# When the weight sums of the Mixer's last product are made, and which engine splits the next weights

## The chip, the cores and the metric

The kernel runs on one core of a Trainium2 chip. The metric is the device time of one execution in microseconds (us), as the median of several runs. Five engines work side by side and meet only at semaphores: TensorE (PE, with its weight loads as PEld), VectorE (DVE), ScalarE (ACT), GpSimd (POOL) and SyncE (SP). Each takes its instructions strictly in the order of its own queue. SP and POOL issue the DMAs here, each on a queue of its own.

## The reference

Two layers, 512 tokens, 1024 features. Each layer is three steps, each with a layer norm (LN) behind it:

```
x = LN(alpha*x + 0.5*swiglu_1(x))
x = LN(alpha*x + Mixer(x))
x = LN(alpha*x + 0.5*swiglu_2(x))

Mixer: zq, zf, zi, zg, zu, zv, za, zb = split(x @ w_in)
  o = hgrn2(q, k, i, log f)               # chunked gated recurrence, 4 heads
  o = o * rsqrt(mean(o^2) + eps) * g * silu(zg);   y_a = o @ w_branch_a
  v = LN(gelu(zv));  mixed = causal 128x128 mixing of v
  y_b = (gelu(zu) * mixed) @ w_branch_b
  y = sigmoid(za)*y_a + sigmoid(zb)*y_b
  return y @ w_out                        # the Mixer's last product
```

All of it is float32. `swiglu` has a hidden width of 2816.

## The kernel before, in words

**Three products for one.** A float32 operand is cut in two by `split` (L125 to L127): ACT copies it, rounded, into `hi`, and DVE subtracts to get `lo`. A product is then three matmuls: hi by hi, hi by lo, lo by hi. `weights` (L129) does this for a weight block of 128x1024: SP loads it into a `raw` tile (four of them), then comes the split, into two of ten `w` tiles or, with `early`, into two of the 34 big tiles of the tag `h`.

**Seven products for eight.** Large products use a scheme of 2x2 blocks with seven products and with sums of blocks on both sides. For the class `Seven` (L295) the sums of weights are made in DRAM, ahead of use: `sums_in_dram` (L308) yields six steps, a copy from DRAM to DRAM and an adding DMA for each of the three kinds of sums (`t13`, `t2`, `t4`). They are issued by POOL, and an add waits on POOL until its copy has landed, the next copy until the add has:

```
for of, kw in ((copy, {}), (add, {"accum_op": ALU.add})):
    for k in ks:
        tc.keep_in_program_order(nc.gpsimd.dma_start(*of(k), **kw))
    yield 0.0, next(gap)
```

Between two steps lies a gap in nanoseconds from a list. For the Mixer's last product that is `OUT_SUMS` (L141), and `w_out` is the source.

**Who sets the order.** `Flow` (L50) keeps a planned clock. Every matmul loop ticks it, and side tasks, written as generators, run one step when they are due: `flow.add(gen, delay)` starts one, `flow.finish` runs one to its end. So the program order, and with it each engine's queue, is woven from a main line and side tasks. Within it a list scheduler may move an instruction ahead on its engine; what `keep_in_program_order` names stays in place.

**The Mixer** (L864 on), main line:
1. queries and gates; `x_sums` forms sums of x; `all_sums` queues the DRAM sums for `two_tokens` and then, as `column_sums` (L932), those for the columns (`zt`, 1 MB each);
2. `columns(4)`: u. A call of `columns` (L941) is seven products with weights loaded by SP;
3. `two_tokens` (L882): i and v by the seven-product scheme. Its order on PE: X and C with b and t1 (`iX`, `iC`), then the copies of X and C out of PSUM by ACT (L905), then `iX` with t2 on the same bank, then c, t3 and t4;
4. v's moments (L1262 to L1272), with four roots `vr` on POOL (`rstd_of`, L185), one for each 128 tokens;
5. `columns(0)` to `columns(3)`: the two gates. Side tasks here: `all_out` with `head_out` (L1161) for pairs of heads (transposes `kt`, states `st`, outputs `o`, roots `rs` on POOL, scaling by DVE, transposes `ot`), and `spatial`, the mixing of v;
6. the loop over k that multiplies both branches, L1313: the products `y`, DVE's gating and sums, and the sums of y for the last product (`activation_sums`, `later`);
7. `so.run` (L424), the last product: b and t2 by P1, P6, P5 (`pA`, `pB`, `pC`), c by P2 and P3, d by P7 and P4 (`pB`, `pF`). DVE adds each bank into x (`add_to`, L200), and `norm` makes LN: mean and square sum, a root on POOL, two passes by DVE (L230, L231). Then PE transposes the new x (`tr`, L177) for the next FFN.

The next FFN begins with four weight blocks, a and b for the blocks 10 and 21, loaded and split by `next_weights` within the Mixer. Before the change, the first two come in the loop over k (at k = 2), the other two in `run`, behind three splits of d.

`first_weights` in `run` is called behind the loads of d for the first two ks (`two_d`, L412, with `early`) and a third:

```
for k in ks[0:early_d]:
    self.two_d(k, True)
if few:
    self.two_d(ks[early_d])
    first = first_weights()
```

`few` is true for the Mixer's last product alone. The sums of `w_out` are started ahead of `two_tokens`, with a delay of 1000 ns.

Of the kernel before, what the change touches and what calls it, by code (L numbers as in the profile page):

```python
# [40 lines left out]
NF = DFF // P  # L41
# [42 lines left out]
def trunk(ctx: ExitStack, tc, x_in, xt_in, w13, w2, w_in, w_iv, w_z, w_br, w_out, ln_g, ln_b, lb_in, hgn, sgg, sgb, sgws,  # L84
# [35 lines left out]
    def pin(ins):  # L120

        if pinned[0]:
            tc.keep_in_program_order(ins)

    def split(hi, lo, src):  # L125
        pin(S.activation(hi, src, AF.Copy))  # L126
        pin(V.tensor_tensor(lo, src, hi.bitcast(F32), op=ALU.subtract))  # L127

    def weights(src, name, early=False):  # L129

        raw = wk.tile([P, D], F32, tag="raw", name=f"r_{name}", bufs=NRAW)
        pin(nc.sync.dma_start(raw, src))
        if early:
            hi, lo = (slot(f"{c}_{name}", F32R).rearrange("p a t -> p (a t)") for c in "hl")
        else:
            hi, lo = (wk.tile([P, D], F32R, tag="w", name=f"{c}_{name}", bufs=NW) for c in "hl")
        split(hi, lo, raw)
        return hi, lo

    SUM_GAP = 7000.0  # L140
    OUT_SUMS = [10000.0, 28000.0, 10000.0, 16000.0, 10000.0, 0.0]  # L141
    X_GAP = 2500.0
# [152 lines left out]
    class Seven:  # L295
# [88 lines left out]

        def two(self, name, loads, keys, early=False):

            m = len(keys)
            raw = wk.tile([P, 2, 512], F32, tag="raw", name=f"r_{name}", bufs=NRAW)
            if len(loads) == 1:
                nc.sync.dma_start(raw[:, 0:m], loads[0])  # L390
            else:
                for z, d in enumerate(loads):
                    nc.sync.dma_start(raw[:, z], d)
            if early:
                hi, lo = (slot(f"{v}_{name}", F32R) for v in "hl")
            else:
                hi, lo = (wk.tile([P, 2, 512], F32R, tag="w", name=f"{v}_{name}", bufs=NW) for v in "hl")
            split(hi[:, 0:m], lo[:, 0:m], raw[:, 0:m])
            for z, key in enumerate(keys):
                self.ops[key] = hi[:, z], lo[:, z]  # L400
# [10 lines left out]

        def two_d(self, k, early=False):  # L412
            self.two(f"d{k}", [self.t13[k][:, 1], self.t4[k]], [("t3", k), ("t4", k)], early)

# [9 lines left out]
        def run(self, c, ln, last, due, first_weights):  # L424
# [64 lines left out]
            for k in ks[0:early_d]:  # L489
                self.two_d(k, True)  # L490
            if few:
# [231 lines left out]

    def ffn_weights(l, i, which=(0, 1)):

        return [[weights(w13[l, i, c + j], f"{n}{j}", True) for n, c in (("a", 0), ("b", NF))]
                for k in FRONT for j in (k + z * NH2 for z in which)]
# [136 lines left out]
    def mixer(l, lb, om, first, next_weights):  # L864
# [372 lines left out]
        def all_out():  # L1237
            for h in range(0, NH, 2):
# [17 lines left out]
                        tril.unsqueeze(1).broadcast_to([P, NH, P]), op=ALU.mult)  # L1256
        flow.finish(in_dram)
        so = Seven(lambda k: w_out[l, k], list(range(KT // 2)), [], "o")
        out_sums = flow.add(so.sums_in_dram(so.order, 4, OUT_SUMS), 1000.0)
        two_tokens()  # L1260
        late.append(flow.add(all_out(), 4000.0))
# [48 lines left out]
        for t in late:  # L1310
            flow.finish(t)
        wbr = [None, None]
        for k in range(4):  # L1313
            for a in range(2):
# [12 lines left out]
            if k < 2:  # L1327
                so.later(k, 0)
                so.later(k, 2)
            if k == 2:  # L1330
                first = next_weights(0)
        flow.finish(out_sums)
        return so.run(1.0 / ALPHA, (l, 1), False, [], lambda: first + next_weights(1))

# [51 lines left out]
    for l in range(DEPTH):  # L1386
        first = ffn(l, 0, first, lambda: mixer_weights(l))
        if l == 0:
            flow.finish(prep)
        first = mixer(l, lb, om, first, lambda z: ffn_weights(l, 1, (z,)))  # L1390
        first = ffn(l, 1, first, (lambda: ffn_weights(l + 1, 0)) if l < DEPTH - 1 else None)
# [98 lines left out]
```

## Time and profile before

| | us |
|---|---|
| median of 3 runs | 2027.38 |
| lowest and highest | 2026.88, 2029.39 |
| the profiled execution | 2028.06 |
| its span, first to last instruction | 2026.3 |
| PE busy | 2002.0 |
| DVE busy | 1699.7 |
| ACT busy | 1072.8 |
| POOL busy | 398.6 |

The span is the time between the first and the last instruction; 1.8 us of the execution lie around it. Mean granted clock of PE is 0.994 of full speed. Views of the profile used here: busy time by engine, by group of instructions and by stretch of time; who waited for whom (the engine that waited, its line, the releaser, total, times, longest); and the timeline (start, duration, engine, line, operation, output from inputs; in brackets the idle time before it and what ended it). Names are those of the program's tiles: `h_` and `l_` are the high and low part, `r_` the raw load; digits at their ends are left out. A busy PE need not be at its peak: its ends are modelled. The Mixer of layer 0 runs from about 352 to 675 us, that of layer 1 from about 1359 to 1683.

### The profile page before, as it was taken

The numbers are of one execution on the slowest core, as the hardware profiler recorded it, in microseconds if no ns is written. First come the engines' busy times: TensorE is split into PE (matmuls) and PEld (weight loads), VectorE is DVE, ScalarE is ACT, GpSimd is POOL, SyncE is SP. The second block draws the span as 40 slices with busy tenths as digits, with TensorE's granted clock in tenths as the row PEclk, the third lists the DMA queues.
The fourth block names the chain that finished last, engine by engine and source line by source line (L and its number), as shares of the span: only waits on it lengthen the run. The fifth ranks groups of instructions, "written<-read, shape, count | busy, mean of one in ns | idle before, by whom it ended". The sixth has DMA issues, their size and how long they took to land. (4 is left out here: it accounts for less than half of the span.)

```text
span 2026.3 us, 34947 instructions
## 1 busy us (share of the span) xinstructions
PE 2002.0 (99%) x13552; PEld 1861.0 (92%) x13552; DVE 1699.7 (84%) x2519; ACT 1072.8 (53%) x1577; POOL 398.6 (20%) x541
## 2 busy tenths in 40 slices
PE   9999999999999999999999999999999999999998
PEld 8999888897998899998899999888889989999986
DVE  8888888976769798888789889889677698988886
ACT  5545665336544464556555456652465454554563
POOL 0322003212200133210123320022222001322101
PEclk9999999999999999999999999999999999999999
DMA  6999786887636389987649997778876363899774
GB/s 237 273 263 241 242 268 228 199 230 237 174 125 214 130 217 255 269 232 259 207 147 283 269 243 260 254 229 206 236 226 166 116 228 113 240 248 265 239 253 135
DMA packets 184006, 448.75 MB, mean 221 GB/s; under 512 B 20480, under 2 KB 20608, under 8 KB 183840
## 3 DMA queue, kind: packets, MB, share of 16 engines
q1 hardware_dynamic: 118656, 271.70, 39.0%
q0 software_dynamic: 65184, 174.82, 35.8%
q8 instruction: 106, 1.74, 0.3%
q14 instruction: 60, 0.49, 0.1%
HBM read 424.42 MB, written 164.63 MB: 291 GB/s over the span
## 5 line engine op out<-in xcount | busy, mean ns | idle before, releaser
L126 ACT ACTIVATE h_pa<-ra 128x1024 fp32r<-128x1024 f32 x80 | 84.5, 1057 | 191.9 <-DVE ra L624 185.9
L322 POOL DMA_DIRECT2D t<-in_w_dram x176 | 145.6, 898 | 202.7 <-DMA t<-in_w_dram 113.4
L127 DVE TENSOR_TENSOR l_pc<-rc,h_pc 128x1024 fp32r<-128x1024 f32 x80 | 97.7, 1222 | 47.7 <-ACT h_pc L126 47.7
L322 POOL DMA_DIRECT2D t<-t x104 | 56.4, 543 | 288.2 <-DMA t<-in_w_dram 260.3
L126 ACT ACTIVATE h_b<-r_b 128x1024 fp32r<-128x1024 f32 (+1 forms) x69 | 71.7, 1042 | 63.5 <-DMA r_b<-t 35.6
L127 DVE TENSOR_TENSOR l_c<-r_c,h_c 128x1024 fp32r<-128x1024 f32 x60 | 72.4, 1222 | 38.9 <-ACT h_c L126 38.1
L127 DVE TENSOR_TENSOR l_b<-r_b,h_b 128x1024 fp32r<-128x1024 f32 (+1 forms) x69 | 83.1, 1205 | 25.2 <-ACT h_b L126 24.9
L127 DVE TENSOR_TENSOR l_pa<-ra,h_pa 128x1024 fp32r<-128x1024 f32 x80 | 97.7, 1221 | 2.6 <-ACT h_pa L126 2.6
L126 ACT ACTIVATE h_c<-r_c 128x1024 fp32r<-128x1024 f32 x60 | 62.6, 1056 | 58.5 <-PE pC L381 33.4
L644 PE MATMUL fC<-xs4h,l_pd 128*128 128x256 f32 x320 | 90.6, 283 | 0.0
L644 PE MATMUL fA<-xh,h_pc 128*128 128x256 f32 x320 | 90.6, 283 | 0.0
L644 PE MATMUL fC<-xs1h,h_pt 128*128 128x256 f32 x320 | 90.6, 283 | 0.0
L644 PE MATMUL fX<-xs2h,l_pa 128*128 128x256 f32 x320 | 90.6, 283 | 0.0
L644 PE MATMUL fX<-xh,h_pa 128*128 128x256 f32 x320 | 90.6, 283 | 0.0
L644 PE MATMUL fC<-xs1h,l_pt 128*128 128x256 f32 x320 | 90.6, 283 | 0.0
L644 PE MATMUL fX<-xl,h_pa 128*128 128x256 f32 x320 | 90.6, 283 | 0.0
L644 PE MATMUL fX<-xs2h,h_pa 128*128 128x256 f32 x320 | 90.6, 283 | 0.0
L644 PE MATMUL fX<-xh,l_pa 128*128 128x256 f32 x320 | 90.6, 283 | 0.0
L644 PE MATMUL fC<-xs1l,h_pt 128*128 128x256 f32 x320 | 90.6, 283 | 0.0
L644 PE MATMUL fX<-xs3h,l_pb 128*128 128x256 f32 x320 | 90.6, 283 | 0.0
L644 PE MATMUL fX<-xs3h,h_pb 128*128 128x256 f32 x320 | 90.6, 283 | 0.0
L644 PE MATMUL fA<-xl,h_pc 128*128 128x256 f32 x320 | 90.6, 283 | 0.0
(480 smaller groups left out, 8018.4 us busy)
## 6 DMA issues: line engine op xcount, KB each, us to landing
t<-in_w_dram POOLq DMA_DIRECT2D x88, 512.0 KB, 9.6
t<-t POOLq DMA_DIRECT2D x104, 256.0 KB, 5.0
t<-in_w_dram POOLq DMA_DIRECT2D x88, 256.0 KB, 7.0
r_c<-in_w_dram SPq DMA_DIRECT2D x44, 512.0 KB, 4.9
r_d<-t SPq DMA_DIRECT2D x88, 256.0 KB, 3.9
ra<-in_w_dram SPq DMA_DIRECT2D x80, 256.0 KB, 5.4
rb<-in_w_dram SPq DMA_DIRECT2D x80, 256.0 KB, 7.4
rc<-in_w_dram SPq DMA_DIRECT2D x80, 256.0 KB, 8.1
```

What stands on the lines that cost most here:

```text
L126: pin(S.activation(hi, src, AF.Copy))
L127: pin(V.tensor_tensor(lo, src, hi.bitcast(F32), op=ALU.subtract))
L322: tc.keep_in_program_order(nc.gpsimd.dma_start(*of(k), **kw))
L644: PE.matmul(ps[:, half[z]], a[:, ms], v, start=start, stop=(m == 3 and i == 2), skip_group_check=not (first and z == 0))
```

## The change

It has three parts.
- The sums of `w_out` start behind `two_tokens` in the program, so behind v's roots in POOL's queue, with a delay of 5000 ns and other gaps.
- The next FFN's weights are loaded and split within the loop over k, one pair at k = 1 and one at k = 2, none in `run`.
- `split` takes the engine of the subtraction as an argument. It is GpSimd for these four blocks and for the two early loads of d in the Mixer's last product. ACT still makes the high parts.

```diff
-    def split(hi, lo, src):
+    def split(hi, lo, src, on=None):
         pin(S.activation(hi, src, AF.Copy))
-        pin(V.tensor_tensor(lo, src, hi.bitcast(F32), op=ALU.subtract))
+        pin((on or V).tensor_tensor(lo, src, hi.bitcast(F32), op=ALU.subtract))
...
-    OUT_SUMS = [10000.0, 28000.0, 10000.0, 16000.0, 10000.0, 0.0]
+    OUT_SUMS = [5000.0, 14000.0, 6000.0, 25000.0, 7000.0, 0.0]
...
             for k in ks[0:early_d]:
-                self.two_d(k, True)
+                self.two_d(k, True, G if few else V)
...
         flow.finish(in_dram)
+        two_tokens()
         so = Seven(lambda k: w_out[l, k], list(range(KT // 2)), [], "o")
-        out_sums = flow.add(so.sums_in_dram(so.order, 4, OUT_SUMS), 1000.0)
-        two_tokens()
+        out_sums = flow.add(so.sums_in_dram(so.order, 4, OUT_SUMS), 5000.0)
         late.append(flow.add(all_out(), 4000.0))
...
         wbr = [None, None]
+        first = []
         for k in range(4):
...
-            if k == 2:
-                first = next_weights(0)
+            if k in (1, 2):
+                first += next_weights(k - 1)
         flow.finish(out_sums)
-        return so.run(1.0 / ALPHA, (l, 1), False, [], lambda: first + next_weights(1))
+        return so.run(1.0 / ALPHA, (l, 1), False, [], lambda: first)
...
-        first = mixer(l, lb, om, first, lambda z: ffn_weights(l, 1, (z,)))
+        first = mixer(l, lb, om, first, lambda z: ffn_weights(l, 1, (z,), G))
```

`weights`, `two` and `ffn_weights` only hand the argument on.

More of the change, by code (lines that the diff above doesn't have):

```diff
@@ L123, in pin, with weights @@
             tc.keep_in_program_order(ins)
-    def split(hi, lo, src):
+    def split(hi, lo, src, on=None):
         pin(S.activation(hi, src, AF.Copy))
-        pin(V.tensor_tensor(lo, src, hi.bitcast(F32), op=ALU.subtract))
-    def weights(src, name, early=False):
+        pin((on or V).tensor_tensor(lo, src, hi.bitcast(F32), op=ALU.subtract))
+    def weights(src, name, early=False, on=None):
         raw = wk.tile([P, D], F32, tag="raw", name=f"r_{name}", bufs=NRAW)
@@ L136, in weights @@
             hi, lo = (wk.tile([P, D], F32R, tag="w", name=f"{c}_{name}", bufs=NW) for c in "hl")
-        split(hi, lo, raw)
+        split(hi, lo, raw, on)
         return hi, lo
     SUM_GAP = 7000.0
-    OUT_SUMS = [10000.0, 28000.0, 10000.0, 16000.0, 10000.0, 0.0]
+    OUT_SUMS = [5000.0, 14000.0, 6000.0, 25000.0, 7000.0, 0.0]
     X_GAP = 2500.0
@@ L383, in mm, with two @@
                 flow.tick(3 * MM)
-        def two(self, name, loads, keys, early=False):
+        def two(self, name, loads, keys, early=False, on=None):
             m = len(keys)
@@ L397, in two @@
                 hi, lo = (wk.tile([P, 2, 512], F32R, tag="w", name=f"{v}_{name}", bufs=NW) for v in "hl")
-            split(hi[:, 0:m], lo[:, 0:m], raw[:, 0:m])
+            split(hi[:, 0:m], lo[:, 0:m], raw[:, 0:m], on)
             for z, key in enumerate(keys):
@@ L410, in two_c, with two_d @@
             self.two(f"c{k}", [self.w_of(k)[:, 2:4]], [("B22", k), ("B21", k)], early)
-        def two_d(self, k, early=False):
-            self.two(f"d{k}", [self.t13[k][:, 1], self.t4[k]], [("t3", k), ("t4", k)], early)
+        def two_d(self, k, early=False, on=None):
+            self.two(f"d{k}", [self.t13[k][:, 1], self.t4[k]], [("t3", k), ("t4", k)], early, on)
         def later(self, k, z):
@@ L722, in trunk, with ffn_weights @@
     FRONT = [10]
-    def ffn_weights(l, i, which=(0, 1)):
-        return [[weights(w13[l, i, c + j], f"{n}{j}", True) for n, c in (("a", 0), ("b", NF))]
+    def ffn_weights(l, i, which=(0, 1), on=None):
+        return [[weights(w13[l, i, c + j], f"{n}{j}", True, on) for n, c in (("a", 0), ("b", NF))]
                 for k in FRONT for j in (k + z * NH2 for z in which)]
```

## The prediction

> **What bounds the kernel now.** The first view is the page's first part, busy time by engine, and with it the list of what TensorE (PE) waited for, whose columns are total us, times and longest.
>
> ```profile
> PE 2002.0 (99%) x13552; PEld 1861.0 (92%) x13552; DVE 1699.7 (84%) x2519; ACT 1072.8 (53%) x1577; POOL 398.6 (20%) x541
> ```
> ```profile
> core 0 of [0], span 2026.3 us
> engine line waited for: us in total, times, longest us
> PE iX L381 <- ACT i L905: 9.2, 2, 4.8
> PE tr L177 <- DVE x L231: 2.7, 2, 1.6
> PE tr L177 <- DVE x L203: 1.5, 2, 0.9
> ```
>
> PE is the bound, and no matmul is added or removed. So only time in which PE stands, or runs at a lower clock after standing, can be won. The three rows hold nearly all waiting that one name explains, once a layer each. `iX` is the product with t2 in `two_tokens`. `tr` are the transposes of the new x at the Mixer's end.
>
> The second view is busy time by stretch: stretch, length, busy time of each engine, granted clock (PEclk), DMA share, GB/s. The first fence is layer 0, the second layer 1.
>
> ```profile
> core 0: us, PE busy (x) PEld busy (x) DVE busy (x) ACT busy (x) POOL busy (x), PEclk, DMA share, GB/s
> 440.00:460.00 20.00, 19.96 (x129) 17.37 (x127) 6.76 (x9) 5.26 (x9) 2.53 (x3) 1.00 1.04 333
> 460.00:465.00 5.00, 0.29 (x1) 0.29 (x2) 3.22 (x6) 2.94 (x4) 2.30 (x3) 0.83 1.07 277
> 465.00:471.00 6.00, 6.00 (x21) 5.06 (x22) 4.22 (x7) 3.78 (x7) 0.00 (x0) 0.57 1.08 286
> ...
> 495.00:560.00 65.00, 65.00 (x550) 64.79 (x549) 51.91 (x79) 39.35 (x68) 19.82 (x27) 1.00 0.61 175
> ...
> 591.00:635.00 44.00, 44.00 (x198) 36.51 (x198) 36.19 (x55) 16.44 (x23) 3.29 (x6) 1.00 0.49 170
> ...
> 651.00:675.00 24.00, 24.00 (x114) 19.76 (x113) 22.44 (x41) 9.73 (x14) 5.57 (x8) 1.00 0.43 143
> 675.00:683.00 8.00, 5.96 (x35) 5.52 (x35) 6.89 (x16) 5.08 (x16) 2.66 (x4) 0.79 1.02 335
> ```
> ```profile
> 1472.00:1478.00 6.00, 5.78 (x20) 4.95 (x21) 4.41 (x7) 4.29 (x8) 0.00 (x0) 0.58 1.08 288
> ...
> 1683.00:1691.00 8.00, 5.82 (x35) 5.22 (x36) 6.55 (x16) 4.74 (x16) 3.14 (x5) 0.79 0.96 320
> ```
>
> Each stall is paid twice: PE stands, then runs at 0.57 or 0.58 of its clock for six microseconds. In `two_tokens` the DMA share is over 1, so transfers are short there. At the Mixer's end it is VectorE (DVE), busy for 22.44 of the 24 us ahead of the stall. The columns (495 to 560) have room: DMA share 0.61.
>
> The third view is the timeline around the first stall, of ScalarE (ACT), then of GpSimd (POOL).
>
> ```profile
> 463.12 1.06 ACT L126 ACTIVATE h_c<-r_c 128x1024 fp32r<-128x1024 f32 x1 [1.98 <-DMA r_c<-in_w_iv_dram]
> 464.08 1.06 ACT L905 ACTIVATE i<-iX 128x512 f32<-128x512 f32 x2
> ```
> ```profile
> 420.44 4.35 POOL L938 DMA_DIRECT2D zt<-in_w_z_dram  x4
> 422.73 4.33 POOL L322 DMA_DIRECT2D o<-in_w_out_dram  x4
> 454.28 1.08 POOL L322 DMA_DIRECT2D o<-in_w_out_dram  x1 [27.21 <-DMA o<-in_w_out_dram]
> ...
> 462.55 1.03 POOL L322 DMA_DIRECT2D o<-in_w_out_dram  x1 [1.89 <-DMA o<-in_w_out_dram]
> ```
>
> PE names L905, the copy that empties its bank. But that copy stands on ACT behind `h_c`, and `h_c` waited for the load of c. The load landed while four copies of w_out's sums landed too: the adds at 454.28 to 462.55 each start when their copy is there. POOL had issued these copies at 422.73, with nothing to hold it, right behind the sums for z. So the stall is contention of the DMA engines with transfers that nobody needs before y ends.
>
> **Part 1: the first portion of the sums leaves `two_tokens`.** It removes from this stretch four copies and four adds of 512 KB each on POOL's DMA queue; SP's loads stay. From 454.28 to 463.12 (8.84 us) loads and copies landed side by side. Without copies I let the loads land in half that time, so `h_c` starts at 458.7 instead of 463.12, 4.4 us earlier. Of a stall of 4.8 us 0.4 us is left, by layer. Bounds: nothing won if the sums for z, which stay, set the pace; all 4.8 if the queue drains faster than by half. I take the half, since loads and copies are equally large. Won: 9.2 - 0.8 = 8.4 us of waiting. The slow clock goes with the stall: 6.00 us at 0.57 and at 0.58 are 2.58 and 2.52 us lost. Part 1 gives 8.4 + 5.1 = **13.5 us**.
>
> A remainder of 0.4 us is taken to cost no clock. The Trainium skill ("TensorE: Matmul & The Clock Gate", Part 1) has the clock halve after an idle window of about 3.4 us. The trace agrees for the 4.8 us stall, but at the Mixer's end no wait of the `tr` rows is over 1.6 us and PEclk still falls to 0.79. By the rule alone that end would hold only its 4.2 us of waiting; the rows decide below.
>
> **Part 2: where the sums go.** They now follow v's roots in POOL's queue. POOL has the copies and adds of t2 there already:
>
> ```profile
> 500.51 2.19 POOL L322 DMA_DIRECT2D o<-o  x4
> ...
> 511.48 0.81 POOL L322 DMA_DIRECT2D o<-in_w_out_dram  x1 [1.62 <-DMA o<-o]
> ...
> 521.89 1.01 POOL L188 TENSOR_TENSOR rs<-rs,mhalf 128x4 f32<-128x4 f32 x1
> ```
> ```profile
> 526.44 1.03 PE L1198 MATMUL ot<-ident,on 128*128 128x128 f32 x8
> ```
>
> The first four copies were issued at 500.51, behind the last of v's roots. After part 1 everything here lies some 7 us earlier, so the first portion goes out at about 493.5. The added wait is that of its four adds for their copies. Behind them on POOL stand the roots `rs` of heads 0 and 1; DVE's scaling and then PE's `ot` wait for those. How long until the last copy has landed? Copies of half the size took 511.48 - 500.51 = 11 us; so 11 to 22 us, and I take 16, near the 2.8 us by copy at 454.28 to 462.55 behind a first latency. The last add then leaves POOL at 510. The roots, done at 522.9 in the old trace, are due at 516, and `ot`, which needs DVE's scaling in between, 3.5 us later at 519.4. Cost zero; even 22 us (add at 515.5, two pairs of roots until 518, scaling until 519) is just covered. The DMA engines have (1 - 0.61) x 65 = 25 us free; four copies at 2.8 us are 11 us at half share, and the adds, which took at most twice that, 22 more: about 17 us of whole engines. SP's loads for the columns are then slower; if that cover were gone, PE would see a stall like today's, up to 4.8 us by layer. The second portion waits for the first's landing and is issued between two pairs of roots; the third is due 55 planned us behind `two_tokens`, at about 543, and `run` starts where y ends, at 635. Cost zero.
>
> **Part 3: low parts on GpSimd, and earlier.** The DVE queue ahead of the end, and what shows of GpSimd beside DVE:
>
> ```profile
> 653.59 3.49 DVE L127 TENSOR_TENSOR l_d<-r_d,h_d 128x1024 fp32r<-128x1024 f32 x3
> 657.00 1.22 DVE L127 TENSOR_TENSOR l_a<-r_a,h_a 128x1024 fp32r<-128x1024 f32 x1
> 658.13 0.68 DVE L203 SCALAR_TENSOR_TENSOR x<-pA,x 128x512 f32<-128x512 f32 x1
> ```
> ```profile
> 718.10 4.49 POOL L823 TENSOR_SCALAR hold<-xs3l 128x1 f32<-128x1 f32 x1 [33.09 <-DVE xs3l L127]
> ```
> ```profile
> 722.45 0.68 DVE L670 TENSOR_TENSOR r<-fC,r 128x512 f32<-128x512 f32 x1
> ```
> ```profile
> 40.55 0.19 POOL L823 TENSOR_SCALAR hold<-xs3l 128x1 f32<-128x1 f32 x1 [38.58 <-DVE xs3l L127]
> ```
> ```profile
> L1057 POOL MEMSET sc<- 128x512 f32 x8 | 4.8, 618 | 20.7 <-PE sp L1070 20.7
> ```
>
> In `run`, DVE loses two of the three `l_d` (3.49 / 3 = 1.16 us each) and `l_a`, `l_b` of the next weights (1.13 us, from 657.00 to 658.13): 4.6 us less ahead of the sums into x, whose norm the transposes wait for. To take away both waits of one layer the norms must come 1.35 + 0.75 = 2.1 us earlier on average (2.7 / 2 and 1.5 / 2).
>
> What comes back: a subtraction of 128x1024 on GpSimd is not in the trace. It is at least DVE's 1.22 us; above, the memset of half the width (0.618 us, one stream) times two for the width and three for two reads and a write gives 3.7 us. I take 2.5, two passes of 1.24, as the two reads are the likeliest limit. And the two engines disturb each other. The same tiny `hold` takes 0.19 us at 40.55 and 4.49 us at 718.10, while DVE runs subtractions and sums from SBUF; it ends at 722.59, just after DVE turns to an operation that reads PSUM (722.45). The trace shows GpSimd waiting for DVE; the reverse no row can show, since all of GpSimd's operations here are tiny. If one of the two `l_d` keeps DVE waiting for 2.5 us and the other lies beside sums that read PSUM, DVE is 4.6 - 2.5 = 2.1 us earlier: just what is needed in the mean, too little in the layer with 1.6 us. I take 85% of the end. The end holds 4.2 us of waiting and (1 - 0.79) x 8 = 1.7 us of clock in each layer: 7.6 us, of which **6.4 us** are won.
>
> Within y, four subtractions of 2.5 us on GpSimd are 10 us. DVE is busy 36.19 of 44 us there, less 2.3 for the two that leave it: 33.9, and 43.9 even if every one kept DVE waiting. It fits, barely, so cost zero; PE has eight banks between itself and DVE. Two loads of the second pair now go out on SP ahead of the last branch weights and hold two of the four raw tiles until GpSimd is done; the x rows and norm parameters queue on POOL behind the subtractions, tens of us before use. Four more of the 34 big slots are taken until the next FFN, so x rows may load later. Zero for each, and a stall of the 1 to 2 us kind if a cover fails.
>
> **Sum.** 13.5 + 6.4 = 19.9 us. The profiled execution took 2028.06 us (span 2026.3), so it would take 2008.2. It lies 0.7 us over the median of the three runs, 2027.38; from that the forecast is **2007.5 us**.
>
> **Rivals.**
> *GpSimd keeps DVE from working* (chance 0.18). Both `l_d` hold DVE up: 4.6 - 5.0 is a loss of 0.4 us, and at 3.7 us each 2.8 us. The end is not won: 2027.38 - 13.5 = 2013.9, or up to 2019.5 if 2.8 us come on top in each layer. For it: the `hold` rows, DVE's 94% ahead of the end. Against: the sums into x read PSUM and leave openings. The Trainium skill ("SBUF — State Buffer", Who interferes with whom) says an operation of DVE with two SBUF inputs and one of GpSimd that reads SBUF exclude each other for a whole instruction, whichever starts first. The `hold` rows agree for one direction, and no run here shows the other.
>
> *Contention stays* (0.08). The sums for z keep the loads late, or the moved portion starves the columns' loads: half of part 1 goes or all of it: 2014 to 2021.
>
> *No change that can be told* (0.04). Both happen: 2023.4 to 2031.4. Less than 0.2%, 4 us, I count as no difference; a measurement of this kernel tells no less.
>
> *Roots behind sums* (0.08), slower. If the copies take as long in the columns as before, 422.73 to 462.55 or 39.8 us, the last add leaves POOL at 533.3 and `ot` comes at 536.5 instead of 519.4: 17 us by layer, 2007.5 + 34 = 2041.5. It costs from 23 us on and makes the kernel slower than before from about 33 us on. For it: POOL works strictly in order. Against: the 39.8 us began behind four transfers for z, and the t2 copies took 11.
>
> **Chances.** The forecast as such has 0.62 (2003 to 2012; 2003 if both places vanish). Faster is 0.62 + 0.18 + 0.08 = 0.88, less 0.01 for the edge: 0.87. Same 0.05, slower 0.08. The range goes from 2003 to 2018: it leaves out the upper part of the first two rivals, no change and slower, together 0.2.
>
> **What would show it.** Right: no `iX` row among PE's waits, PEclk 1.00 throughout `two_tokens`, POOL's first `o` copies behind the last `vr`, roots `rs` within 3 us of their input, `l_a` and `l_b` on POOL, x's first sum no later than 2 us after its product. Wrong: a wait of `ot` for `on`, subtractions on DVE that start late while a POOL subtraction runs, or `tr` still waiting for x.

## The result and the profile after

| | before | after |
|---|---|---|
| median of 4 runs, us | 2027.21 | 2038.4 |
| lowest and highest | 2026.88, 2029.39 | 2037.29, 2042.38 |
| profiled span | 2026.3 | 2035.4 |

The ratio is 1.0051 (95% interval 1.0039 to 1.0064). The change makes the kernel 10.3 us slower (0.0051 x 2027.2) where 20 us faster was forecast. The page's first part and the list of PE's waits, after:

```profile
PE 2001.7 (98%) x13552; PEld 1860.1 (91%) x13552; DVE 1701.4 (84%) x2507; ACT 1072.5 (53%) x1577; POOL 431.3 (21%) x553
```
```profile
PE pa L156 <- ACT xh L126: 12.8, 3, 6.3
PE pa L156 <- DVE xl L127: 3.4, 2, 1.7
PE y L156 <- ACT h_br L126: 3.2, 2, 1.6
PE y L156 <- DVE l_br L127: 2.2, 2, 1.1
```

PE does the same work. The wait of `iX` for ACT, 9.2 us before, is gone. In its place stand two new ones: `y`, the products of the branches, waits for their weights `br` (5.4 us in both layers), and `pa`, the first product of the next FFN, waits for `xh` and `xl`, the split of the new x (16.2 us). Before, the end of the Mixer held 4.2 us of waiting, put down to `tr`.

The same stretches by busy time (stretch, length, PE, PEld, DVE, ACT, POOL, granted clock, DMA share, GB/s), layer 0:

```profile
460.00:465.00 5.00, 5.00 (x27) 4.28 (x27) 4.54 (x8) 4.62 (x8) 0.00 (x0) 1.00 0.70 233
465.00:471.00 6.00, 6.00 (x28) 4.95 (x27) 3.28 (x4) 3.21 (x4) 0.00 (x0) 1.00 0.83 274
488.00:553.00 65.00, 65.00 (x550) 64.81 (x549) 50.51 (x77) 38.37 (x67) 26.13 (x34) 1.00 0.82 216
584.00:628.00 44.00, 41.30 (x177) 33.42 (x175) 32.90 (x45) 15.99 (x21) 12.22 (x6) 0.96 0.29 107
628.00:644.00 16.00, 16.00 (x72) 13.28 (x71) 13.98 (x20) 8.61 (x11) 2.10 (x4) 1.00 1.00 354
674.00:690.00 16.00, 8.82 (x58) 8.42 (x59) 11.43 (x25) 8.12 (x27) 4.60 (x6) 0.79 0.72 244
```

The first two rows are `two_tokens`: no gap and full clock, where before PE was busy for 0.29 of 5 us and then ran at 0.57. The third is the columns, which now carry the copies and adds: DMA share 0.82 instead of 0.61, and PE without a gap. So the first half of the change does what it was to do. The fourth is y: PE stands for 2.7 us, the clock falls to 0.96, and the DMA engines have little to do (0.29 for 0.49 before). The fifth, the start of `run`, then has them full. The last is the end of the Mixer: 8.82 us busy of 16 at 0.79.

**Why y waits.** SP's queue in y (start, duration, queue, line, output from input, count):

```profile
575.28 0.33 SPq L132 DMA_DIRECT2D r_a<-in_w_dram  x1
578.16 0.33 SPq L132 DMA_DIRECT2D r_b<-in_w_dram  x1
581.04 3.21 SPq L132 DMA_DIRECT2D r_br<-in_w_br_dram  x2
586.84 0.33 SPq L132 DMA_DIRECT2D r_a<-in_w_dram  x1
594.88 0.33 SPq L132 DMA_DIRECT2D r_b<-in_w_dram  x1
614.13 3.15 SPq L132 DMA_DIRECT2D r_br<-in_w_br_dram  x2
```

From 594.88 to 614.13 SP issues nothing. Four raw tiles exist, and from 594.88 all four hold next weights: the first pair (575.28, 578.16) and the second (586.84, 594.88). The last branch weights need one. When do the first come free? ACT's queue, with the idle time before in brackets:

```profile
608.68 0.63 ACT L126 ACTIVATE tm<-s 128x512 fp32r<-128x512 f32 x1 [5.94 <-DVE s L353]
...
610.53 1.04 ACT L126 ACTIVATE h_a<-r_a 128x1024 fp32r<-128x1024 f32 x1
...
617.66 1.06 ACT L126 ACTIVATE h_br<-r_br 128x1024 fp32r<-128x1024 f32 x1 [0.65 <-DMA r_br<-in_w_br_dram]
```

The first pair was loaded at 575 to 578 and is split at 610.53. ACT had time, 5.94 us of it right before 608.68, but the split stands behind other pinned work in its queue, at the place where the program wrote it. GpSimd's subtraction `l_a`, which reads the tile last, ends at 614.11 (611.66 + 2.45, shown in the last section); SP has the tile at 614.13, and `h_br` waits for that load at 617.66.

### The profile page after: what moved, and what is told of

The parts are those of the page before. It is cut to its first block, busy times and chain, and to the rows that moved or that the text cites. A ratio compares the mean times of both kernels' runs of the same rounds, so it can differ in the third digit from the quotient of the medians.

```text
span 2035.4 us, 34941 instructions
## 1 busy us (share of the span) xinstructions
PE 2001.7 (98%) x13552; PEld 1860.1 (91%) x13552; DVE 1701.4 (84%) x2507; ACT 1072.5 (53%) x1577; POOL 431.3 (21%) x553
## 5 line engine op out<-in xcount | busy, mean ns | idle before, releaser
L127 DVE TENSOR_TENSOR l_b<-r_b,h_b 128x1024 fp32r<-128x1024 f32 (+1 forms) x65 | 78.4, 1206 | 27.9 <-ACT h_b L126 27.8
L644 PE MATMUL fA<-xh,l_pc 128*128 128x256 f32 x320 | 90.6, 283 | 0.0
L644 PE MATMUL fX<-xs2l,h_pa 128*128 128x256 f32 x320 | 90.6, 283 | 0.0
L644 PE MATMUL fC<-xs4h,h_pd 128*128 128x256 f32 x320 | 90.6, 283 | 0.0
L644 PE MATMUL fC<-xs4l,h_pd 128*128 128x256 f32 x320 | 90.6, 283 | 0.0
```

The lines of the kernel that those rows point to most:

```text
L127: pin((on or V).tensor_tensor(lo, src, hi.bitcast(F32), op=ALU.subtract))
L644: PE.matmul(ps[:, half[z]], a[:, ms], v, start=start, stop=(m == 3 and i == 2), skip_group_check=not (first and z == 0))
```

## The experiments

One measure is used for all: the time lost by PE. It is the time from one matmul's start to the next, less the time that the same shape takes undisturbed, summed over a stretch where it is over 0.02 us; it holds the waiting and the slow clock, and it comes from one profiled execution of each kernel. The slow clock comes in steps of up to 1.7 us (last section), so a difference of 1 to 2 us in one layer may be a single step. "Versus before" is the ratio less one, times 2027.2 us; it is given because the runs of the kernel before, made side by side with each, had medians of 2027.2 to 2031.3.

| kernel | versus before, us | ratio | lost in y, by layer | lost at the end |
|---|---|---|---|---|
| before | | | 0, 0 | 4.5, 4.5 |
| after | +10.3 | 1.0051 | 4.8, 4.6 | 10.6, 10.5 |
| e1_sums | -13.4 | 0.9934 [0.9919, 0.9949] | 0, 0 | 4.5, 6.2 |
| e3_dve_early | +2.6 | 1.0013 [1.0003, 1.0023] | 4.3, 4.4 | 7.3, 7.9 |
| e4_d_gpsimd | -4.3 | 0.9979 [0.9970, 0.9989] | 0, 0 | 9.4, 9.5 |
| e5_next_gpsimd | +2.0 | 1.0010 [1.0000, 1.0019] | 4.7, 4.8 | 7.2, 7.0 |
| e6_after_loads | -9.1 | 0.9955 [0.9940, 0.9969] | 0, 0 | 5.1, 5.0 |
| e8_g_after_loads | +12.8 | 1.0063 [1.0046, 1.0080] | 0, 0 | 11.3, 11.5 |
| e9_d_no_sub | -11.1 | 0.9945 [0.9930, 0.9960] | 0, 0 | 6.9, 7.3 |
| e11_xr_last | -11.4 | 0.9944 [0.9929, 0.9959] | 0, 0 | 5.2, 5.1 |
| e12_k0_k2 | -14.6 | 0.9928 [0.9916, 0.9941] | 0, 0 | 4.9, 4.9 |
| e12_xr_last | -13.4 | 0.9934 [0.9922, 0.9947] | 0, 0 | 5.7, 5.0 |
| e14_d_xr_last | -8.7 | 0.9957 [0.9944, 0.9971] | 0, 0 | 8.1, 7.4 |
| e17_five_raw | +11.6 | 1.0057 [1.0041, 1.0072] | 0, 0 | 7.0, 7.9 |
| e18_fixed_order | -12.0 | 0.9941 [0.9928, 0.9953] | 0, 0 | 6.6, 6.3 |
| e18f_mean_first | -15.2 | 0.9925 [0.9913, 0.9938] | 0, 0 | 5.3, 5.3 |
| e19_fixed_d_gpsimd | -10.5 | 0.9948 [0.9935, 0.9961] | 0, 0 | 7.3, 7.7 |
| e20_fixed_run_pair | -15.4 | 0.9924 [0.9910, 0.9937] | 0, 0 | 4.8, 4.3 |
| e21_bad_order | -10.9 | 0.9946 [0.9933, 0.9958] | 0, 0 | 6.6, 5.7 |
| e22_good_order | -8.5 | 0.9958 [0.9945, 0.9971] | 0, 0 | 9.0, 7.9 |

### The change taken apart

The first four kernels each keep a part of the change. `e1_sums` has the moved sums alone; `split` and the next weights are as before.

> The change's first half alone: w_out's sums move behind v's roots with the new delays; the next weights and the two d stay as before, on VectorE. Theory A (the moved sums win what was forecast, GpSimd's subtractions lose more): the stall of iX behind L905 is gone in both layers, no new stall in y, the Mixer's end as in the kernel before with 4 to 4.5 us per layer; 13.5 us faster than before, 2013 to 2015. Rival B (the sums, now within the columns and y, cause the new stall in y): y stalls here too by 5 us per layer, and the time is 2022 to 2026.

It gains 13.4 us; y loses nothing, and the end about what it lost before (its `tr` waits are 2.9 and 1.8 us, before 2.7 and 1.5). The 1.7 us more in layer 1 are slow clock for the most part: it is half for 6.83 us there, for 3.41 us in layer 0 and before the change.

`e3_dve_early` is the whole change with every subtraction back on DVE:

```diff
-                self.two_d(k, True, G if few else V)
+                self.two_d(k, True)
...
-        first = mixer(l, lb, om, first, lambda z: ffn_weights(l, 1, (z,), G))
+        first = mixer(l, lb, om, first, lambda z: ffn_weights(l, 1, (z,)))
```

> The change with every subtraction left on VectorE: sums moved, next weights split within y after k 1 and 2, nothing on GpSimd. Theory A: VectorE frees the raw tiles at once, so y's stall is gone (under 1 us per layer), and the Mixer's end, relieved of l_a and l_b (2.4 us of VectorE), waits 2 to 4 us per layer less than before: 2006 to 2012. Rival B (the earlier loads alone fill the four raw tiles, whichever engine subtracts): the stall of 5 us per layer in y remains, and the time is 2018 to 2024. Rival C (the end is late because the new order of VectorE's work there is worse, not because of GpSimd): the end loses 5 us or more per layer against the kernel before, 2020 or more.

A miss: it is 16.0 us slower than `e1_sums` (0.0079 x 2027.2), and y stalls without GpSimd. So GpSimd is not the cause of that stall. `e4_d_gpsimd` adds to `e1_sums` only the two early d on GpSimd:

```diff
-                self.two_d(k, True)
+                self.two_d(k, True, G if few else V)
```

> Sums moved, next weights as before, and only the two d of the Mixer's end subtracted on GpSimd. Theory A (GpSimd's subtraction keeps VectorE standing for 2.4 to 2.8 us each): no stall in y, and the end at least as late as in the changed kernel, 10 to 12 us of lost time per layer against 4.5 before, so 10 to 16 us over the kernel with moved sums alone: 2024 to 2030. Rival (two d on GpSimd are neutral or a gain, and the end was spoilt by the next weights): at most the time of the kernel with moved sums alone, 2008 to 2014.

It is 9.1 us slower than `e1_sums`, nearly all at the end. The time is in the range of the first reading; the loss at the end, 9.4 and 9.5 us, is a little under its 10 to 12:

```profile
PE pa L156 <- ACT xh L126: 10.2, 2, 5.1
```

`e5_next_gpsimd` is the change with d back on DVE, so GpSimd has only the four next weights:

```diff
-                self.two_d(k, True, G if few else V)
+                self.two_d(k, True)
```

> The change without the two d on GpSimd: sums moved, the next weights' low parts on GpSimd within y. Theory A: the stall in y stays in full, 5 us per layer, since four subtractions of 2.5 to 3.4 us one behind another hold the raw tiles; the end is better than before by 1 to 4 us per layer: 2014 to 2022. Rival (y's stall needs the two d as well): y free, 2006 to 2012.

The stall of y is as expected, the time is a miss: 2014 to 2022 was expected with a better end, and the end got worse (7.2 and 7.0 us). The kernel stands beside `e3_dve_early`: +2.0 and +2.6. Which engine subtracts the next weights makes no difference here; when they are loaded does. The parts add up: -13.4 (sums), +16.0 (weights earlier), +9.1 (d on GpSimd) make +11.7, against +10.3 measured.

### The stall of y: who holds the raw tiles

If the four raw tiles are the cause, the stall must go without touching GpSimd's part or the weights' count, once SP gets a tile in time. Three ways were tried. `e6_after_loads` (all on DVE) issues the second pair only behind the loads of the last branch weights:

```diff
+                if (k, a) == (3, 0):
+                    first += next_weights(1)
...
-            if k in (1, 2):
-                first += next_weights(k - 1)
+            if k == 1:
+                first += next_weights(0)
```

> Everything on VectorE, sums moved, first pair of next weights behind k 1 as in the change, second pair only behind the loads of the last branch weights (in k 3). Theory D (in the change the four raw tiles all hold next weights from the last split of k 2's branch weights until the engines reach the place of the first pair, so k 3's branch weights load 20 us late; that stall also delays the loads of c and d and so the Mixer's end): y is free of its stall of 4.4 us per layer, c lands in time, and the end waits no more than in the kernel with moved sums alone; 2006 to 2015. Rival E (any early splitting in y starves it): the stall stays, 2025 or more. Rival F (the end is set by the order in which ScalarE's and VectorE's work there was queued, which is the changed one here too): y free, but the end at 7 us per layer instead of 4.5: 2018 to 2022.

Nothing is lost in y, and the kernel is 11.8 us faster than `e3_dve_early` (0.0058 x 2027.2). The mechanism is that of the first reading; the time, 2020.51, misses its 2006 to 2015 and lies in the range of the third, whose 7 us at the end did not come (5.1 and 5.0). `e12_k0_k2` (all on DVE) only spreads the two pairs:

```diff
-            if k in (1, 2):
-                first += next_weights(k - 1)
+            if k in (0, 2):
+                first += next_weights(k // 2)
```

> Everything on VectorE, sums moved, first pair of next weights behind k 0, second behind k 2, so that each pair has given its two raw tiles back before they are wanted. Theory D (raw tiles): y has no stall (after k 0 the first pair gives its tiles back at about 600, 17 us before k 3's branch weights are used), run's loads of b are as early as in the kernel with moved sums alone, and the end has 2.4 us less of VectorE ahead of it: 2008 to 2014, at least as fast as the kernel with moved sums alone. Rival F (the queued order at the end eats the relief): y free, end 5 to 7 us per layer, 2015 to 2020. Rival E (any early splitting starves y): 2025 or more.

The stretch of y in its trace, against 41.30 of 44 us after:

```profile
584.00:628.00 44.00, 44.00 (x200) 36.61 (x199) 36.84 (x57) 18.42 (x24) 2.19 (x4) 1.00 0.52 171
```

At -14.6 us it beats both kernels; 2014.29 is at the edge of the expected range. `e17_five_raw` leaves the order of `e3_dve_early` and gives a fifth raw tile, paid for with one big slot:

```diff
-    NS, NRAW, NSA = 34, 4, 3
+    NS, NRAW, NSA = 33, 5, 3
```

> The change with everything on VectorE (which stalled y by 4.4 us per layer) and five raw tiles instead of four, paid for with one of the 34 big slots; nothing else is moved. Theory D: with one tile more the first of k 3's two branch weights loads some 18 us earlier, the second still waits for the first pair: y's stall falls from 4.4 to 1 to 3 us per layer, 2 to 7 us under the same kernel with four: 2022 to 2029. Rival E (the stall is of splitting on ScalarE and VectorE, not of tiles): y's stall as before, 2029 to 2033.

The time is a miss, but y answers the question. SP's queue, the stretch of y, and one of PE's waits:

```profile
600.75 6.37 SPq L132 DMA_DIRECT2D r_br<-in_w_br_dram  x2
```
```profile
584.00:634.00 50.00, 50.00 (x247) 42.45 (x247) 38.74 (x58) 21.06 (x27) 2.20 (x4) 1.00 0.47 148
```
```profile
PE fX L644 <- ACT r L664: 17.5, 4, 5.4
```

The last branch weights go out at 600.75, in `e3_dve_early` at 612.75, although y starts 6 us later here (590.19 and 584.07); and y has no gap. What the kernel loses it loses in the four FFNs, where a big slot is missing: `fX` waits there for 17.5 us, and with the slow clock behind each wait 27 us are lost (7.9, 7.5, 7.0 and 4.6).

`e8_g_after_loads` is the change with GpSimd kept and the second pair moved as in `e6_after_loads`:

> The change as it is, GpSimd included, with only the second pair of next weights moved behind the loads of the last branch weights. Theory D: y's stall goes although GpSimd still does all its subtractions there, 8 to 10 us less than the change: 2027 to 2031; what is left over the kernel with moved sums alone is the Mixer's end. Rival (GpSimd's subtractions themselves stall y through VectorE): 2034 or more.

A miss: slower than the change itself (+12.8). The tiles are free and y loses nothing, but the second pair's subtractions on GpSimd now lie over the start of `run`. First POOL, then DVE:

```profile
626.54 2.49 POOL L127 TENSOR_TENSOR l_a<-r_a,h_a 128x1024 fp32r<-128x1024 f32 x1 [10.11 <-ACT h_a L126]
632.38 2.41 POOL L127 TENSOR_TENSOR l_b<-r_b,h_b 128x1024 fp32r<-128x1024 f32 x1 [3.35 <-ACT h_b L126]
```
```profile
626.69 2.88 DVE L127 TENSOR_TENSOR tl<-s,th 128x512 fp32r<-128x512 f32 x1
...
633.28 2.59 DVE L127 TENSOR_TENSOR l_b<-r_b,h_b 128x1024 fp32r<-128x1024 f32 x1 [0.85 <-ACT h_b L126]
```

DVE's `tl` takes 2.88 us where the same shape takes 0.68, and `l_b` 2.59 for 1.22. The first products of `run` wait for that `l_b` (6.5 us in two waits, 3.50 and 3.03), and 6.6 and 5.7 us are lost there. So GpSimd's subtraction cost nothing where DVE had time to spare, in y, and it costs much here.

### The end of the Mixer

Three questions: is the relief of DVE worth anything, what does GpSimd cost, and does the order of the queues matter?

**The relief.** In `e12_k0_k2` DVE has two subtractions less ahead of the norms than in `e1_sums`; otherwise their ends agree. The prediction counts on such relief. The two DVE queues, `e1_sums` first:

```profile
646.74 3.49 DVE L127 TENSOR_TENSOR l_d<-r_d,h_d 128x1024 fp32r<-128x1024 f32 x3
...
653.67 0.21 DVE L216 TENSOR_SCALAR nm<-sums 128x1 f32<-128x1 f32 x1
...
671.77 0.20 DVE L216 TENSOR_SCALAR nm<-sums 128x1 f32<-128x1 f32 x1
```
```profile
648.03 3.49 DVE L127 TENSOR_TENSOR l_d<-r_d,h_d 128x1024 fp32r<-128x1024 f32 x3
...
652.66 1.22 DVE L127 TENSOR_TENSOR l_d<-r_d,h_d 128x1024 fp32r<-128x1024 f32 x1
653.80 0.21 DVE L216 TENSOR_SCALAR nm<-sums 128x1 f32<-128x1 f32 x1
...
655.31 1.41 DVE L230 SCALAR_TENSOR_TENSOR x<-x,nm,lng 128x512 f32<-128x512 f32 x2 [0.70 <-ACT sq L219]
657.20 1.41 DVE L231 SCALAR_TENSOR_TENSOR x<-x,rstd,lnb 128x512 f32<-128x512 f32 x2 [0.47 <-POOL rstd L188]
...
671.62 0.20 DVE L216 TENSOR_SCALAR nm<-sums 128x1 f32<-128x1 f32 x1
```

`nm` is a token's mean. The first is taken at 653.80 instead of 653.67, the last at 671.62 instead of 671.77. PE is 0.4 us later in `e12_k0_k2` (its last `pF` starts at 667.29, in `e1_sums` at 666.88), so counted from PE the first mean is 0.3 us earlier and the last 0.6 (in layer 1 the last is 1.1 earlier): of 2.4 us less work a quarter to a half arrives. The three `l_d` start 1.3 us later, and the fourth now stands ahead of the first mean, in the place of `l_b`. Between means DVE waits 0.70 us for ACT's squares and 0.47 for POOL's root, with a token about every 6 us: each step holds waits for two other engines beside DVE's own work.

`e9_d_no_sub` is `e4_d_gpsimd` with the subtraction taken out: the low parts of the two early d are a second copy by ACT, so they aren't the reference's, and neither DVE nor GpSimd works on them.

```diff
-            split(hi[:, 0:m], lo[:, 0:m], raw[:, 0:m], on)
+            if on is G:
+                S.activation(hi[:, 0:m], raw[:, 0:m], AF.Copy)
+                S.activation(lo[:, 0:m], raw[:, 0:m], AF.Copy)
+            else:
+                split(hi[:, 0:m], lo[:, 0:m], raw[:, 0:m])
```

> The kernel with only the two d moved off VectorE, but their low parts come from a second copy on ScalarE instead of a subtraction on GpSimd (so these low parts are not the reference's). VectorE is relieved by 2.4 us and GpSimd runs nothing beside it. Theory G (GpSimd's two subtractions keep VectorE standing, and this makes the end late): the end gets better than with moved sums alone, 2 us per layer and more: 2005 to 2014. Rival F (the changed order of ScalarE's and VectorE's queues makes the end late: copies xr ahead of the next token's xh): no better than 2 us under the kernel with the two d on GpSimd, 2020 to 2026.

It answers neither way cleanly, also because ACT has two copies more. Even with both subtractions gone, the kernel isn't faster than `e1_sums` (0.9945 and 0.9934): no win of the relief shows here either. Against `e4_d_gpsimd` 6.9 us come back by the ratios, 4.3 by the spans; so GpSimd's own part in the 9.1 us is about 4 to 7 us, and the rest comes with what else differs from `e1_sums`, the order of ACT's queue among it.

**GpSimd on DVE.** In `e4_d_gpsimd`, POOL and then DVE:

```profile
643.73 2.40 POOL L127 TENSOR_TENSOR l_d<-r_d,h_d 128x1024 fp32r<-128x1024 f32 x1 [15.54 <-PE pC L381]
648.26 2.47 POOL L127 TENSOR_TENSOR l_d<-r_d,h_d 128x1024 fp32r<-128x1024 f32 x1 [2.13 <-ACT h_d L126]
```
```profile
644.80 1.88 DVE L127 TENSOR_TENSOR s<-r,s 128x512 fp32r<-128x512 f32 x1
...
648.40 3.42 DVE L127 TENSOR_TENSOR l_d<-r_d,h_d 128x1024 fp32r<-128x1024 f32 x1
```

DVE's `l_d` starts at 648.40, while POOL's runs until 648.26 + 2.47 = 650.73; it ends at 651.82, 1.09 us after that, and alone it takes 1.22. So it stood still until GpSimd was done. The `s` took 1.88 for 0.68. Together 3.4 us are lost to DVE against 2.4 relieved. The last mean comes at 674.77, 3.0 us later than in `e1_sums`, 2.5 counted from the last `pF` (667.35 and 666.88).

**The order.** In the change, ACT's queue at the end, and below it that of the kernel before:

```profile
677.80 0.66 ACT L182 ACTIVATE xr<-tr 128x256 f32<-128x256 f32 x2 [3.42 <-DVE xl L127]
678.34 1.38 ACT L126 ACTIVATE xh<-tr 128x256 fp32r<-128x256 f32 x4
```
```profile
674.60 0.38 ACT L126 ACTIVATE xh<-tr 128x256 fp32r<-128x256 f32 x1 [0.45 <-PE tr L177]
677.29 0.38 ACT L126 ACTIVATE xh<-tr 128x256 fp32r<-128x256 f32 x1 [2.30 <-PE tr L177]
677.57 0.66 ACT L182 ACTIVATE xr<-tr 128x256 f32<-128x256 f32 x2
```

Before, the `xh` of the next two tokens stand ahead of the copies `xr` of the first; after, `xr` stands first, waits 3.42 us for DVE's `xl`, and the four `xh` wait behind it. The list scheduler chose that order, and a wait for `xh` of like length stands in `e4_d_gpsimd`, where only the engine of two subtractions changed. Is it the cause? `e11_xr_last`, `e12_xr_last` and `e14_d_xr_last` put a token's `xr` behind all its `xh`, on `e6_after_loads`, `e12_k0_k2` and `e4_d_gpsimd`:

```diff
+        plain = []
...
-            for r in range(2):
-                S.activation(xr[2 * q + r][:, :, ts], pv[:, r], AF.Copy)
+            plain += [(xr[2 * q + r][:, :, ts], pv[:, r]) for r in range(2)]
+        for to, of in plain:
+            S.activation(to, of, AF.Copy)
```

> The kernel with the second pair behind the loads, everything on VectorE, and in addition the copies xr of a token emitted behind all four xh of the token, everywhere in the kernel. Theory F (an xr copy that waits for VectorE stands ahead of xh on ScalarE and TensorE waits for xh): the end falls to 2 to 4 us per layer, 3 to 8 us under the same kernel without this edit: 2004 to 2014. Rival (the end is set by VectorE's sums and norms alone): within 2 us of the same kernel without this edit.

> The same with the copies xr of a token behind its four xh. Theory F: the end falls by 1 to 3 us per layer against the same kernel without this edit: 2005 to 2012. Rival: within 2 us of it.

> Only the two d on GpSimd, next weights as before, sums moved, and the copies xr of a token behind its four xh. Theory F (the 5.2 us wait for xh at the end comes of the xr copies queued ahead of it): the end falls from 9.4 to 5 to 7 us per layer, 4 to 8 us under the kernel with the two d on GpSimd: 2016 to 2021. Theory G (VectorE, kept standing by GpSimd, is late for xl, and any order waits for that): the end stays at 9 us or more, 2023 to 2027.

The first two make no difference that can be told: -11.4 for -9.1, -13.4 for -14.6, intervals overlapping. The third wins 4.5 us of the 9.1 by the ratios (0.9957 for 0.9979), in the range of the first reading, but its end stays over the 5 to 7 us expected, for much of the waiting moves: `tr` now waits for `xr`, 7.8 us in two waits, where `pa` waited 13.3.

`e21_bad_order` takes `e1_sums` and forces the change's order on ACT alone, without any work for GpSimd (the `xh` of tokens 1 and 2 behind the `xr` of token 0); `e22_good_order` takes `e4_d_gpsimd` and puts the `xr` of token 0 behind the first `xh` of token 1:

```diff
+            if held[0] and t in (1, 2) and q == 0:
+                with tc.issue_after(held[1].ins):
+                    for hlp in halves:
+                        split(*hlp)
```
```diff
+            made = S.activation(halves[0][0], halves[0][2], AF.Copy)
+            if held[0] and (t, q) == (1, 0):
+                with tc.issue_after(made.ins):
+                    for to, of in held[1]:
+                        S.activation(to, of, AF.Copy)
```

> The kernel with moved sums alone, everything on VectorE as before, and only ScalarE's order at the Mixer's end changed to the change's: the first halves xh of tokens 1 and 2 queued behind the copies xr of token 0. Theory F (this order makes the end late): TensorE waits for xh 4 to 6 us per layer in one piece, and the kernel is 4 to 10 us slower than with moved sums alone: 2018 to 2025. Theory G (it was GpSimd): within 3 us of the kernel with moved sums alone, 2012 to 2018.

> The kernel with the two d on GpSimd, and only ScalarE's order changed: the copies xr of token 0 queued behind token 1's first xh. Theory F: the wait for xh of 5.1 us goes, and the kernel is 3 to 8 us faster than with the two d on GpSimd in the scheduler's order: 2016 to 2021. Theory G: 2022 to 2027.

The forced order brings the wait of the change back, in a kernel in which GpSimd subtracts nothing:

```profile
PE pa L156 <- ACT xh L126: 8.2, 2, 4.2
```

But it costs only 2.4 us against `e1_sums` (0.0012 x 2027.2; 0.6 by the spans), for much of that waiting replaces the `tr` waits; the two intervals overlap. So the wait is as the first reading had it, the time as the second. The good order wins 4.3 us back from `e4_d_gpsimd`, as the first reading had it; here too much of the waiting moves, to `tr` behind `xr` (8.6 us in two waits). So the order costs at most 1 to 2 us a layer; of the 1.6 us that layer 1 loses less with the good order, some 1.1 are a shorter fall of the clock (3.41 us instead of 6.83).

**A fixed order.** Four kernels write DVE's order at the end by hand (`pin_last` keeps an instruction at its place), so that relief and GpSimd can be weighed in one order: the next token's sums stand between the two passes of a norm.

```diff
+                pin_last(add_to(xs[t], 0, c, B[tt]))
+                norm_scale(xs[t - 1], n1[0], g)
                 mm(F, P4, ks[-tail:], tt, True, True)
+                norm_shift(t - 1, xs[t - 1], n1[1], b, 11500.0 - 2 * 2592.0)
+                pin_last(add_to(xs[t], 0, c, F[tt], sums[t]))
+                n1 = norm_head(xs[t], sums[t])
```

`e18_fixed_order` is `e12_k0_k2` so ordered; `e18f_mean_first` takes the next mean ahead of `norm_shift`; `e19_fixed_d_gpsimd` adds the two d on GpSimd to `e18_fixed_order`; `e20_fixed_run_pair` is `e1_sums` in this order, without relief.

> The kernel with the pairs behind k 0 and k 2, everything on VectorE, and at the Mixer's end VectorE's work fixed by hand: sums of the next token between a token's two norm steps, token after token. Theory H (the end is a chain: mean, square on ScalarE, root on GpSimd, two norm steps, and a token's mean waits in VectorE's order behind the whole norm of the token before): the means come 1 to 2 us earlier per token, the end falls from 4.9 to 1 to 3 us per layer, 4 to 8 us under the same kernel in the scheduler's order: 2006 to 2011. Rival I (VectorE's busy time is the limit, whatever the order): within 2 us of it, 2013 to 2016.

> The same with the next token's mean ahead of the second norm step of the token before. Theory H: the last token's norm ends another 1 us earlier, 2005 to 2011, within 2 us of the other fixed order. Rival I: 2013 or more.

> The same fixed order, but the two d on GpSimd. Theory G (GpSimd's two subtractions keep VectorE standing): VectorE's d is stretched from 1.2 to 3.4 us again, the first means are 1 to 3 us later, and the kernel is 3 to 8 us slower than the fixed order with all on VectorE. Rival F (it was the order alone): within 2 us of it.

> The same fixed order, next weights as in the kernel before (second pair split at the Mixer's end by VectorE, 2.4 us more of its work there). Theory H says the chain has slack for it only in part: 0 to 3 us slower than the fixed order with the pairs in y. If the relief was worth what the forecast took it for, 5 us and more slower.

The hand-made order wins nothing from the relief: with it 0.9941, without it (`e20_fixed_run_pair`) 0.9924, and each of the five times without is under each of the five with. The expectations had it the other way: `e18_fixed_order` was to be 4 to 8 us faster than `e12_k0_k2` or within 2 of it and is 2.4 slower, `e20_fixed_run_pair` was to be slower than `e18_fixed_order` and is 3.3 faster. That the scheduler's order eats the relief, which I had come to think, falls. Taking the mean first is as fast as the best (0.9925), which is the rival's range. GpSimd in one and the same order costs 0.7 and 1.4 us of lost time by layer, less than a step of the clock; the ratios, 0.9948 and 0.9941, can't tell that apart, and 1.6 us between the medians is what the rival of `e19_fixed_d_gpsimd` said.

## Why the prediction was wrong, step by step

**Part 1 was right.** `h_c` starts at 458.15; 458.7 was forecast. The `iX` row is gone and the clock stays at 1.00. `e1_sums` measures 13.4 us; the sum said 13.5. The interval goes from 10.3 to 16.4, so that it agrees to 0.1 us is luck.

**Part 2 was right.** POOL's queue behind v's roots:

```profile
492.64 2.32 POOL L322 DMA_DIRECT2D o<-in_w_out_dram  x4
...
508.33 1.03 POOL L322 DMA_DIRECT2D o<-in_w_out_dram  x1 [1.18 <-DMA o<-in_w_out_dram]
511.81 0.19 POOL L187 TENSOR_SCALAR rs<-ms 128x4 f32<-128x4 f32 x1 [2.44 <-DVE ms L1190]
```

The copies go out at 492.64 (forecast 493.5), the last add ends at 509.4 (510), and the first roots then wait for their own input, not for the sums. The rival of roots behind sums did not come.

**Part 3 failed, at two steps.** The first is "Two loads of the second pair now go out on SP ahead of the last branch weights and hold two of the four raw tiles until GpSimd is done", with "Zero for each". It counts the second pair alone. The first pair held the other two, and the end of GpSimd's subtraction came late because the split came up in ACT's queue only at 610.53, 35 us after the load was issued. The waits are of the 1 to 2 us kind that the text feared (1.6 and 1.1, the longest), but there are two a layer and a slow clock behind them: y loses 4.7 us a layer. In `e3_dve_early` the start of `run`, whose loads queue behind, loses 1.7 and 2.0 more, and the end 7.3 and 7.9 for 4.9 and 4.9 in `e12_k0_k2`, which differs from it only in the place of the two pairs; by the ratios that place is worth 17.2 us (0.0085 x 2027.2). `e6_after_loads`, `e12_k0_k2` and `e17_five_raw` show the mechanism from three sides.

The second is the 6.4 us that "are won" at the Mixer's end, by "4.6 - 2.5 = 2.1 us earlier". DVE's balance came out much as counted. GpSimd's subtraction takes 2.40 and 2.47 us in `e4_d_gpsimd`, 2.41 and 2.80 in the change (2.5 was taken). The rival "GpSimd keeps DVE from working" came true in part: in the change the two cost DVE 0.5 us (an `s` of 1.17 us for 0.68, while sums that read PSUM run free) and 2.2 us (an `l_d` of 3.42 us). That is 2.7 together, so 1.9 of the 4.6 us are left. But the norms did not come earlier. The last mean is taken 8.6 us behind the start of the last `pF` matmul (680.16 and 671.54), before the change 4.7 us (678.40 and 673.74); in layer 1 it is 8.5 and 5.3 us. What failed is the step from DVE's balance to the norms: a relief does not arrive there whole, and something else came late.

Counted from the last `pF` in the same way, three pairs of kernels give the parts, for layers 0 and 1. The relief alone makes the last mean 0.6 and 1.1 us earlier (`e12_k0_k2` against `e1_sums`), GpSimd on the two d 2.5 and 2.0 us later (`e4_d_gpsimd` against `e1_sums`), the early place of the pairs 2.3 and 2.9 us later (`e3_dve_early` against `e12_k0_k2`). Together that is 4.2 and 3.8 us later; measured are 4.0 and 3.2. The last of the three is the stall of y once more. The loads of c stand behind y's in SP's queue, and in the change the first goes out 38.2 us ahead of that `pF` (633.33), before it 43.1 us (630.60). ACT's third `h_c` then waits 2.12 us for its load, and DVE for that `h_c`:

```profile
647.33 1.23 DVE L127 TENSOR_TENSOR l_c<-r_c,h_c 128x1024 fp32r<-128x1024 f32 x1 [1.96 <-ACT h_c L126]
```

Even the relief that arrives wins nothing for PE that can be told: by the ratios `e12_k0_k2` is 1.2 us better than `e1_sums`, with an uncertainty of some 4 us, and it loses 4.9 and 4.9 us at the end for 4.5 and 6.2; in the fixed order the kernel without relief is the faster one.

Lost at the end are 10.6 and 10.5 us a layer instead of 4.5: 12.1 us more, where 6.4 less were forecast. Nearly all of it is waiting: 16.2 us by the rows of `pa`, where `tr` had waited 4.2. The rival's price of 2.8 us a layer was too low, as it held neither the late loads nor the order of ACT's queue.

The forecast for the profiled execution was 2008.2 us, and it took 2037.29. Of these 29.1 us, y's 9.4 and the end's 18.5 (12.1 + 6.4) make 27.9. Open is how the end's 6 us a layer divide: about 1 to 4 are GpSimd's hold on DVE (`e19_fixed_d_gpsimd`; `e4_d_gpsimd` against `e22_good_order` and `e21_bad_order`), at most 1 to 2 the order, and 2 to 3 come with the place of the pairs (`e3_dve_early` against `e12_k0_k2`). For these last the clock is most of it: over 16 us of the end the granted clock is 0.79 in both layers of `e3_dve_early`, 0.89 and 1.00 in `e12_k0_k2`, which makes about 1.6 and 3.2 us. Why it is slow for longer there no run isolates.

## What to carry to other kernels

Before a load is moved ahead, list every load that holds a buffer of its ring at that time, each until its consumer's place in the queue, not until its data are there: a consumer pinned behind other work keeps the buffer although its engine idles. Work taken off a busy engine wins time only as far as that engine's load sets the step; where its queue shows short waits for other engines between the steps, count on a part, and look for what else comes late. Change one engine and a list scheduler may reorder others, so compare the order of all queues before reading a gain or loss as that of the engine; here the better kernel is the change without GpSimd and with the two pairs behind k = 0 and k = 2, or simply the moved sums alone (0.9928 and 0.9934, not distinguishable).

## What the runs showed of the hardware

**GpSimd holds DVE for a whole instruction.** The prediction had rows for one direction only. In the change, DVE beside the first of the four subtractions on POOL in y:

```profile
611.66 2.45 POOL L127 TENSOR_TENSOR l_a<-r_a,h_a 128x1024 fp32r<-128x1024 f32 x1 [59.16 <-ACT h_a L126]
614.08 2.85 POOL L127 TENSOR_TENSOR l_b<-r_b,h_b 128x1024 fp32r<-128x1024 f32 x1
616.89 2.55 POOL L127 TENSOR_TENSOR l_a<-r_a,h_a 128x1024 fp32r<-128x1024 f32 x1
```
```profile
612.48 2.18 DVE L1326 TENSOR_TENSOR r<-z,z 128x512 f32<-128x512 f32 x1
615.14 2.07 DVE L127 TENSOR_TENSOR tl<-r,th 128x256 fp32r<-128x256 f32 x1 [0.48 <-ACT th L126]
617.13 0.68 DVE L1324 TENSOR_TENSOR z<-z,y 128x512 f32<-128x512 f32 x1
```

`r`, with two inputs from SBUF, takes 2.18 us (0.68 alone, as in `e8_g_after_loads` at 622.76): POOL's `l_a` ends at 614.11, and 0.55 us later `r` is done. `z<-z,y`, which reads PSUM, takes its usual 0.68 while POOL's next subtraction runs beside it (616.89 to 619.44). The Trainium skill ("SBUF — State Buffer", Who interferes with whom) has a DVE instruction with two SBUF inputs and a GpSimd instruction that reads SBUF block each other in full, whoever comes first winning. The trace agrees, now in both directions.

**The clock falls after short waits, in whole steps.** In y no wait of the rows is over 1.6 us, yet the granted clock of those 44 us is 0.96. Cut where the clock falls, the stretch reads:

```profile
617.33:620.74 3.41, 0.89 (x3) 0.46 (x4) 2.47 (x3) 1.30 (x2) 3.41 (x2) 1.00 0.50 172
620.74:624.15 3.41, 3.41 (x9) 2.65 (x10) 2.95 (x3) 1.54 (x2) 3.14 (x3) 0.50 0.49 154
```

Two waits (1.62 and 1.08 us) leave PE 0.89 us of work in 3.41 us; then the clock is half for 3.41 us, in which PE is busy throughout, so 1.7 us are lost. Half for 3.41 of 44 us is the 0.96. Every fall within the Mixers of these traces lasts 3.41 or 6.83 us, and 3.41 us cost at most 1.7, less where PE waits within them; the 0.57 before the change is such a fall of 6.83 us (463.27 to 470.10), seen in a stretch that holds 5.1 us of it. The same loss need not bring a step: both layers of `e12_k0_k2` lose 4.9 us at the end, one with a fall of 3.41 us, the other with none. The Trainium skill ("TensorE: Matmul & The Clock Gate", Part 1) asks for an idle window of about 3.4 us; the trace differs, as it did at the Mixer's end before.
